# Instance norm over rows of 4096: one-pass statistics on VectorE for three rows of a tile, ScalarE takes the fourth

## The chip, the cores and the metric

The kernel runs on one core of one Trainium2 chip. The metric is device time in microseconds; before the change it is 4962.84 us, the median of three runs between 4960.73 and 4963.6.

## The reference

```python
batch, channels, length = 256, 256, 4096
x = np.random.randn(batch, channels, length).astype(np.float32)
eps = np.float32(1e-5)

def reference(x, eps):
    mean = np.mean(x, axis=2, keepdims=True)
    var = np.var(x, axis=2, keepdims=True)
    return ((x - mean) / np.sqrt(var + eps)).astype(np.float32)
```

There are 256 x 256 = 65,536 independent rows of 4096 floats. Each row needs its mean and its variance, and then one pass that subtracts and scales. Input and output are 1073.74 MB each.

## The kernel before

A tile is 128 partitions with K = 4 rows each: 512 rows, 64 KiB per partition, 8.39 MB in all. There are 128 tiles. Three buffers X[0] to X[2] hold tiles in SBUF; a tile is loaded into a buffer, normalised in place and stored from the same buffer. Nothing else of size is kept in SBUF; the output of the passes that are only summed goes to `junk` in PSUM.

Four engines run programs of their own, joined by semaphores that are written by hand:

- SyncE issues every DMA on one queue. In its loop (lines 202 to 205) it waits until tile t is done, issues its store (`store`, L164), waits until the store of tile t - 1 has landed, and issues the load of tile t + 2 into that buffer (`load`, L169). So the queue carries store, load, store, load, in that order, whole tiles at a time. Tile 0 is loaded, computed and stored in halves of two rows (L193, L180), and the last tile is stored in halves (L180).
- VectorE runs `vector_tile` once per tile. When the load has landed it takes four row sums (L89), each of which raises `means`. For each pair of rows it then waits for the standard deviations, takes their reciprocals (L97), forms the bias -mean/std (L99), and normalises the rows in place (L111): rows 0, 1 and 2 whole, and the last 1024 elements of row 3.
- ScalarE runs `scalar_tile`. For each row it waits for the row's sum and takes one Square pass over (sum - 4096 x) with an accumulated result (L136), which is the variance up to a factor; after each pair it takes the square root (L145). Finally it waits for `scaled` and normalises the first Q = 3072 elements of row 3 (L150).
- GpSimd only waits at the end for the last stores.

`done[s]` counts the finished pieces of a tile: K + 1 = 5 of them let the store go. The helper `take` (lines 67 to 69) waits for a semaphore and clears it, so that waits through it are shown under L69.

Of the kernel before, what the change touches and what calls it, by code (L numbers as in the profile page):

```python
# [10 lines left out]
def kernel(  # L11
# [6 lines left out]
    nc = tc.nc  # L18
    fp32 = mybir.dt.float32
    AX = mybir.AxisListType  # L20
    AF = mybir.ActivationFunctionType
    ALU = mybir.AluOpType
    P = 128
    K = 4
    BUFS = 3
    Q = 3072
# [2 lines left out]
    out_flat = out.flatten_outer_dims()  # L29
    n, d = x_flat.shape  # L30
    assert n % (P * K) == 0 and d & (d - 1) == 0

    ntiles = n // (P * K)
    x_t = x_flat.rearrange("(t p k) d -> t p k d", p=P, k=K)
# [3 lines left out]
    half = K // 2  # L38

    pool = ctx.enter_context(tc.tile_pool(name="pool", bufs=1))  # L40
# [2 lines left out]

    eps_tile = pool.tile([P, 1], fp32)

    junk = psum.tile([P, d], fp32)
    X = [pool.tile([P, K, d], fp32, name=f"x{s}") for s in range(BUFS)]
    total, ss, std, rstd, nbias = (
        [pool.tile([P, K], fp32, name=f"{name}{s}") for s in range(BUFS)]
        for name in ("total", "ss", "std", "rstd", "nbias")  # L50
    )
# [4 lines left out]
    loaded = [nc.alloc_semaphore(f"loaded{s}") for s in range(BUFS + 1)]  # L56
    stored = [nc.alloc_semaphore(f"stored{s}") for s in range(BUFS + 1)]
    own_v = nc.alloc_semaphore("own_v")
    own_a = nc.alloc_semaphore("own_a")
    means = nc.alloc_semaphore("means")  # L60
    stds = nc.alloc_semaphore("stds")
    scaled = nc.alloc_semaphore("scaled")
    done = [nc.alloc_semaphore(f"done{s}") for s in range(BUFS + 1)]
    ready = nc.alloc_semaphore("ready")
    issued = nc.alloc_semaphore("issued")

    def take(engine, sem, count):
        engine.wait_ge(sem, count)
        engine.sem_clear(sem)  # L69

    V, A, S, G = nc.vector, nc.scalar, nc.sync, nc.gpsimd

    def vector_tile(s, r0=0, k=K, ld=None, dn=None):

        x = X[s]
        ld = loaded[s] if ld is None else ld
        dn = done[s] if dn is None else dn
        dn = dn if isinstance(dn, list) else [dn] * K
        own = 0

        def mine(instruction):
            nonlocal own
            own += 1
            return instruction.then_inc(own_v, 1)

        if ld:
            take(V, ld, 16)
        for r in range(r0, r0 + k):
            V.reduce_sum(out=total[s][:, r : r + 1], in_=x[:, r, :], axis=AX.X).then_inc(means, 1)  # L89
        for b in range(r0, r0 + k, 2):  # L90
            c = slice(b, b + 2)
            final = b == r0 + k - 2
            if final:
                take(V, stds, (b - r0) // 2 + 1)
            else:
                V.wait_ge(stds, (b - r0) // 2 + 1)
            mine(V.reciprocal(out=rstd[s][:, c], in_=std[s][:, c]))  # L97
            V.wait_ge(own_v, own)
            mine(V.scalar_tensor_tensor(  # L99
                out=nbias[s][:, c], in0=total[s][:, c], scalar=-1.0 / d, in1=rstd[s][:, c], op0=ALU.mult, op1=ALU.mult  # L100
            ))
            if final:
                take(V, own_v, own)
            else:
                V.wait_ge(own_v, own)
            if final:
                V.sem_inc(scaled, 1)
            for r in range(b, b + 2):
                c = slice(r, r + 1)
                f = slice(Q, d) if r == r0 + k - 1 else slice(0, d)  # L110
                V.tensor_scalar(  # L111
                    out=x[:, r, f], in0=x[:, r, f], scalar1=rstd[s][:, c], scalar2=nbias[s][:, c],
                    op0=ALU.mult, op1=ALU.add,
                ).then_inc(dn[r], 1)

    def scalar_tile(s, r0=0, k=K, ld=None, dn=None):

        x = X[s]
        dn = done[s] if dn is None else dn
        last = r0 + k - 1  # L120
        own = 0

        def mine(instruction):
            nonlocal own
            own += 1
            return instruction.then_inc(own_a, 1)

        for r in range(r0, last + 1):
            c = slice(r, r + 1)
            if own:  # L130
                A.wait_ge(own_a, own)
            if r == last:
                take(A, means, k)
            else:
                A.wait_ge(means, r - r0 + 1)
            mine(A.activation(  # L136
                out=junk, in_=x[:, r, :], func=AF.Square, bias=total[s][:, c], scale=-float(d), accum_out=ss[s][:, c]
            ))
            if (r - r0) % 2:
                c = slice(r - 1, r + 1)  # L140
                if r == last:
                    take(A, own_a, own)
                else:
                    A.wait_ge(own_a, own)
                A.activation(  # L145
                    out=std[s][:, c], in_=ss[s][:, c], func=AF.Sqrt, bias=eps_tile, scale=1.0 / d**3
                ).then_inc(stds, 1)
        c = slice(last, last + 1)
        take(A, scaled, 1)
        A.activation(  # L150
            out=x[:, last, :Q], in_=x[:, last, :Q], func=AF.Identity, bias=nbias[s][:, c], scale=rstd[s][:, c]
        ).then_inc(dn, 1)

    def rows_of(ap, t):

        if isinstance(t, int):
            return ap[t]
        first, period, count, i = t
        ap = ap[first : first + period * (count - 1) + 1 : period]
        return ap[bass.ds(i, 1)].rearrange("o p k d -> p (o k) d")  # L160

    def store(s, t):
        take(S, done[s], K + 1)
        S.dma_start(out=rows_of(out_t, t), in_=X[s][:, :, :]).then_inc(stored[s], 16)  # L164

    def load(s, t, wait=True):
        if wait:
            take(S, stored[s], 16)
        S.dma_start(out=X[s][:, :, :], in_=rows_of(x_t, t)).then_inc(loaded[s], 16)  # L169

    def half_of(h):
        return slice(h * half, (h + 1) * half)

    def second(sems, s, h):
        return sems[BUFS] if h else sems[s]

    def store_half(s, t, h, count=half + 1):
        r = half_of(h)
        take(S, second(done, s, h), count)
        S.dma_start(out=out_t[t][:, r, :], in_=X[s][:, r, :]).then_inc(second(stored, s, h), 16)  # L180

    def halves(tile_fn, s):
        for h in range(2):
            tile_fn(s, h * half, half, second(loaded, s, h), second(done, s, h))

    last = ntiles - 1
    rounds = (ntiles - 5) // BUFS
    L0 = 2

    with tc.tile_critical():  # L190
        for h in range(2):
            r = half_of(h)
            S.dma_start(out=X[0][:, r, :], in_=x_t[0][:, r, :]).then_inc(second(loaded, 0, h), 16)  # L193
        load(1, 1, wait=False)
        store_half(0, 0, 0)
        store_half(0, 0, 1)
        load(2, 2, wait=False)
        store(1, 1)
        take(S, stored[BUFS], 16)
        load(0, 3)  # L200

        with S.Fori(0, rounds) as i:
            for t in range(L0, L0 + BUFS):
                store(t % BUFS, (t, BUFS, rounds, i))
                load((t + 2) % BUFS, (t + 2, BUFS, rounds, i))
        load(last % BUFS, last)
        store((last - 2) % BUFS, last - 2)
        store((last - 1) % BUFS, last - 1)
        store_half(last % BUFS, last, 0, half)
        store_half(last % BUFS, last, 1)  # L210
        S.sem_inc(issued, 1)
        take(G, issued, 1)
        for s in ((last - 2) % BUFS, (last - 1) % BUFS, last % BUFS, BUFS):
            take(G, stored[s], 16)

        V.memset(eps_tile, eps).then_inc(ready, 1)  # L216
        halves(vector_tile, 0)
        vector_tile(1)
        with V.Fori(0, rounds) as i:  # L219
            for j in range(BUFS):  # L220
                vector_tile((L0 + j) % BUFS)
        vector_tile((last - 2) % BUFS)
        vector_tile((last - 1) % BUFS)
        vector_tile(last % BUFS, dn=[done[last % BUFS]] * half + [done[BUFS]] * half)

        take(A, ready, 1)
        halves(scalar_tile, 0)
        scalar_tile(1)
        with A.Fori(0, rounds) as i:
            for j in range(BUFS):  # L230
                scalar_tile((L0 + j) % BUFS)
        scalar_tile((last - 2) % BUFS)
        scalar_tile((last - 1) % BUFS)
        scalar_tile(last % BUFS, dn=done[BUFS])


# [33 lines left out]
```

## Time and profile before

| | before |
|---|---|
| time, median of 3 | 4962.84 us |
| span of the profiled execution | 4959.6 us |
| DVE busy (VectorE) | 3292.8 us, 66%, 1537 instructions |
| ACT busy (ScalarE) | 2406.0 us, 49%, 1411 instructions |
| row sums, L89, DVE | 512 x 4412 ns |
| Square passes, L136, ACT | 512 x 3679 ns, and 187 ns for each read of the accumulator |
| normalising, L111, DVE | 383 x 2411 ns (4096 elements) and 129 x 808 ns (1024) |
| normalising, L150, ACT | 129 x 2950 ns (3072 elements) |
| roots, L145, ACT | 256 x 296 ns |
| reciprocals L97 and biases L99, DVE | 256 x 159 ns and 256 x 161 ns |

Busy time is that of instructions on an engine; what an engine spends in waits is not in it. The DMA has rows of its own on the page: the share of the sixteen DMA engines in forty equal slices of the span as tenths (9 means 90% or more), and for each queue the packets, the megabytes and the share of sixteen engines' span that the packets took. A row of the waits names who waited, for whom, the total, the count and the longest. A row of the table by stretches gives the stretch and its length, the busy time of DVE, ACT and POOL with the number of instructions, the granted clock, the DMA share and the GB/s.

### The profile page before, as it was taken

The page shows a single profiled execution, that of the slowest core. Times are in us where ns is not written, and L with a number is a line of the kernel's source. Part 1 is how long each engine was busy: PE and PEld are TensorE (multiplying, and loading weights), DVE is VectorE, ACT ScalarE, POOL GpSimd, SP SyncE. Part 2 cuts the span into 40 slices and gives each one's busy share as a digit, 9 for nine tenths or more (in the row PEclk, how much of TensorE's full clock was granted, in tenths as well). Part 3 has the DMA queues.
Part 4 walks back from the last instruction along what each step waited for, and adds up shares of the span by engine and source line. Part 5 has one row for each costly group of instructions (what it writes and reads, how often), then busy time and mean ns, then how long its engine had stood idle before and what let it go on. Part 6 is the DMA issues. An engine that isn't in the chain of part 4 may idle for free.

```text
span 4959.6 us, 5426 instructions
## 1 busy us (share of the span) xinstructions
DVE 3292.8 (66%) x1537; ACT 2406.0 (49%) x1411; POOL 0.2 (0%) x4
## 2 busy tenths in 40 slices
DVE  6666666666666666666666666666666666666666
ACT  4455444554445544455445544455444554445544
POOL 0000000000000000000000000000000000000000
DMA  9999999999999999999999999999999999999999
GB/s 422 431 431 432 434 432 431 437 434 431 436 434 432 436 434 433 436 433 436 434 433 436 434 432 436 434 433 435 434 433 436 433 433 437 433 433 436 434 432 413
DMA packets 37298, 2147.52 MB, mean 433 GB/s; under 512 B 4144, under 2 KB 4144, under 8 KB 4144
## 3 DMA queue, kind: packets, MB, share of 16 engines
q1 hardware_dynamic: 37296, 2147.50, 100.0%
q14 instruction: 2, 0.02, 0.0%
HBM read 1073.74 MB, written 1073.74 MB: 433 GB/s over the span
## 4 chain that ended last, share of the span: by engine, by line
DVE 62%; another core or an unknown queue 31%; issue 4%; DMA 2%; DVEq 0%; ACT 0%; SPq 0%; ACTq 0%
DVE total L89 44%; DVE x L111 17%; DMA x<-in_x_dram 1%; DVE nbias L99 1%; DMA out_dram<-x 1%; DVE rstd L97 1%; DVEq L69 0%; ACT junk L136 0%; DVEq L219 0%; ACT L145 0%; ACT std L145 0%; ACTq L69 0%; SPq L69 0%; SPq L265 0%
## 5 line engine op out<-in xcount | busy, mean ns | idle before, releaser
L89 DVE TENSOR_REDUCE total<-x 128x1 f32<-128x4096 f32 x512 | 2227.0, 4412 | 1591.6 <-DMA x<-in_x_dram 1591.6
L136 ACT ACTIVATE junk<-x,total 128x4096 f32<-128x4096 f32 x512 | 1883.6, 3679 | 2361.8 <-DVE total L89 2361.8
L111 DVE TENSOR_SCALAR x<-x,rstd,nbias 128x4096 f32<-128x4096 f32 (+1 forms) x512 | 1005.9, 2007 | 28.7 <-DVE nbias L99 24.0
L150 ACT ACTIVATE x<-x,nbias,rstd 128x3072 f32<-128x3072 f32 x129 | 380.6, 2950 | 145.0 <-DVEq L69 145.0
L136 ACT ACTIVATION_READ_ACCUMULATOR junk<-x,total 128x1 f32 x512 | 95.8, 187 | 0.0
L145 ACT ACTIVATE std<-ss,eps_tile 128x2 f32<-128x2 f32 x256 | 75.9, 296 | 19.0
L97 DVE RECIPROCAL rstd<-std 128x2 f32<-128x2 f32 x256 | 40.7, 159 | 10.3 <-ACT std L145 10.3
L99 DVE SCALAR_TENSOR_TENSOR nbias<-total,rstd 128x2 f32<-128x2 f32 x256 | 41.2, 161 | 8.8
L136 ACT ACT_TABLE_LOAD x1 | 1.3, 1283 | 1.2 <-DVE eps_tile L216 1.2
L145 ACT ACT_TABLE_LOAD x1 | 1.3, 1283 | 0.1
L216 DVE MEMSET eps_tile<- 128x1 f32 x1 | 0.1, 59 | 1.0 <-SPq L190 1.0
L251 POOL MEMSET const-bfloat16-1.0<- 128x1 bf16 x1 | 0.1, 103 | 0.0
L251 POOL MEMSET const-uint8-127<- 128x1 uint8 x1 | 0.1, 103 | 0.0
L251 POOL MEMSET const-float32-1.0<- 128x1 f32 x1 | 0.1, 100 | 0.0
L251 POOL MEMSET const-float32-0.0<- 128x1 f32 x1 | 0.1, 99 | 0.2 <-issue 0.2
## 6 DMA issues: line engine op xcount, KB each, us to landing
out_dram<-x SPq DMA_DIRECT2D x4, 4096.0 KB, 20.5
x<-in_x_dram SPq DMA_DIRECT2D x2, 4096.0 KB, 16.7
x<-in_x_dram SPq DMA_DIRECT2D x127, 50.3
out_dram<-x SPq DMA_DIRECT2D x126, 31.6
```

The source lines that it names most:

```text
L89: V.reduce_sum(out=total[s][:, r : r + 1], in_=x[:, r, :], axis=AX.X).then_inc(means, 1)
L97: mine(V.reciprocal(out=rstd[s][:, c], in_=std[s][:, c]))
L99: mine(V.scalar_tensor_tensor(out=nbias[s][:, c], in0=total[s][:, c], scalar=-1.0 / d, in1=rstd[s][:, c], op0=ALU.mult, op1=ALU.mult))
L111: V.tensor_scalar(out=x[:, r, f], in0=x[:, r, f], scalar1=rstd[s][:, c], scalar2=nbias[s][:, c], op0=ALU.mult, op1=ALU.add,).then_inc(dn[r ...
L136: mine(A.activation(out=junk, in_=x[:, r, :], func=AF.Square, bias=total[s][:, c], scale=-float(d), accum_out=ss[s][:, c]))
L145: A.activation(out=std[s][:, c], in_=ss[s][:, c], func=AF.Sqrt, bias=eps_tile, scale=1.0 / d**3).then_inc(stds, 1)
L150: A.activation(out=x[:, last, :Q], in_=x[:, last, :Q], func=AF.Identity, bias=nbias[s][:, c], scale=rstd[s][:, c]).then_inc(dn, 1)
L216: V.memset(eps_tile, eps).then_inc(ready, 1)
L251: nc = _bacc.Bacc("TRN2", target_bir_lowering=False, num_devices=1)
```

## The change

Two new functions, `vector_whole` and `scalar_whole`, take the place of `vector_tile` and `scalar_tile` for every tile but tile 0, which keeps the old ones in halves.

VectorE takes mean and variance of rows 0, 1 and 2 in one pass each: eight statistics instructions on 512 elements, and one that combines the eight results into mean and variance. ScalarE takes row 3 alone, and starts on it as soon as VectorE tells it through `started` that the load has landed: one Identity pass that accumulates the mean, and one Square pass for the variance. The square roots of row 3, of rows 0 and 1 together, and of row 2 are taken by ScalarE. VectorE forms the first three scales and biases together, takes row 2's statistics after them, and then normalises the first 3072 elements of row 3 and the whole of row 2. ScalarE normalises the whole of row 0, row 1 in two parts, and the last 1024 elements of row 3. The purpose is to divide the work so that neither engine waits for the other's statistics of every row, and to read each row of VectorE once for both moments.

A tile now has six pieces, and the store waits for K + 2. The last tile's first half waits for three.

```diff
+    R = d - Q
+    F = nc.vector.BN_STATS_FMAX
+    chunks = d // F
+    stats = pool.tile([P, K - 1, chunks, nc.vector.BN_STATS_DIM], fp32)
+    mv = [pool.tile([P, K, nc.vector.BN_AGGR_DIM], fp32, name=f"mv{s}") for s in range(BUFS)]
...
+    def vector_whole(s, dn=None):
...
+        def statistics(r):
+            for f in range(chunks):
+                mine(V.bn_stats(out=stats[:, r, f, :], in_=x[:, r, f * F : (f + 1) * F]))
+            V.wait_ge(own_v, own)
+            V.bn_aggr(out=mv[s][:, r + 1, :], in_=stats[:, r, :, :]).then_inc(means, 1)
...
+        take(V, loaded[s], 16)
+        V.sem_inc(started, 1)
+        statistics(0)
+        statistics(1)
+        c = slice(0, K - 1)
+        V.wait_ge(stds, 2)
+        scales(c)
+        mine(V.scalar_tensor_tensor(
+            out=nbias[s][:, c], in0=mv[s][:, c, 0], scalar=-1.0, in1=rstd[s][:, c], op0=ALU.mult, op1=ALU.mult
+        ))
+        V.wait_ge(own_v, own)
+        V.sem_inc(scaled, 1)
+        statistics(2)
+        normalise(K - 1, slice(0, Q), dn[1])
+        take(V, stds, 3)
+        mine(V.reciprocal(out=rstd[s][:, K - 1 :], in_=std[s][:, K - 1 :]))
+        take(V, own_v, own)
+        normalise(2, slice(0, d), dn[1])
...
+    def scalar_whole(s, dn=None):
...
+        take(A, started, 1)
+        A.activation(
+            out=junk, in_=last, func=AF.Identity, scale=1.0 / d, accum_out=mv[s][:, 0:1, 0]
+        ).then_inc(own_a, 1)
+        A.wait_ge(own_a, 1)
+        A.activation(
+            out=junk, in_=last, func=AF.Square, bias=mv[s][:, 0:1, 0], scale=-1.0, accum_out=ss[s][:, 0:1]
+        ).then_inc(own_a, 1)
+        take(A, own_a, 2)
+        root(slice(0, 1), ss[s][:, 0:1], 1.0 / d)
+        A.wait_ge(means, 2)
+        root(slice(1, K - 1), mv[s][:, 1 : K - 1, 1], 1.0)
+        take(A, scaled, 1)
+        normalise(0, slice(0, d), dn[0])
+        normalise(1, slice(0, R), dn[0])
+        take(A, means, 3)
+        root(slice(K - 1, K), mv[s][:, K - 1 :, 1], 1.0)
+        normalise(1, slice(R, d), dn[0])
+        normalise(K - 1, slice(Q, d), dn[1])
...
-        take(S, done[s], K + 1)
+        take(S, done[s], K + 2)
...
-        store_half(last % BUFS, last, 0, half)
+        store_half(last % BUFS, last, 0)
...
-                vector_tile((L0 + j) % BUFS)
+                vector_whole((L0 + j) % BUFS)
...
-                scalar_tile((L0 + j) % BUFS)
+                scalar_whole((L0 + j) % BUFS)
```

In both functions `normalise` works on one row: VectorE's subtracts the mean and multiplies by the scale, ScalarE's multiplies by the scale and adds the bias. The columns of `mv`, `std`, `rstd` and `nbias` are shifted by one, so that row 3 has column 0 and rows 0, 1 and 2 have columns 1, 2 and 3.

## Prediction

> **What bounds the kernel now.** I read the page's DMA rows first, because the engine rows (DVE 66%, ACT 49%) leave room on both engines, then what the engines and the DMA queue wait for, then one tile in the timeline. The rows of the page's parts 2 and 3:
>
> ```profile
> DMA  9999999999999999999999999999999999999999
> ...
> q1 hardware_dynamic: 37296, 2147.50, 100.0%
> ...
> HBM read 1073.74 MB, written 1073.74 MB: 433 GB/s over the span
> ```
>
> The packets of the one queue fill the sixteen DMA engines' whole span, from the first slice to the last, and the bytes are exactly one read of x and one write of the result: nothing is moved twice. The longest waits (total, times, longest):
>
> ```profile
> ACT junk L136 <- DVE total L89: 2361.8, 512, 18.3
> DVE total L89 <- DMA x<-in_x_dram: 1591.6, 126, 13.7
> ```
>
> VectorE waits 1591.6/126 = 12.6 us per tile for a load; ScalarE's wait for row sums lies inside VectorE's own work. Two stretches of one tile, engines idle and engines at work (length, busy DVE, ACT, POOL, clock, DMA share, GB/s):
>
> ```profile
> 2008.60:2020.90 12.30, 0.00 (x0) 0.00 (x0) 0.00 (x0) 1.00 0.98 426
> 2021.00:2047.00 26.00, 25.70 (x12) 18.75 (x11) 0.00 (x0) 1.00 1.01 439
> ```
>
> While no engine works, the DMA still moves 426 GB/s. The same tile in the timeline of the SyncE queue:
>
> ```profile
> 2008.58 0.34 SPq L164 DMA_DIRECT2D out_dram<-x  x1
> 2009.16 0.35 SPq L169 DMA_DIRECT2D x<-in_x_dram  x1
> 2047.15 0.34 SPq L164 DMA_DIRECT2D out_dram<-x  x1
> ```
>
> From issue to landing, in the answers for the loop's stores (L164), its loads (L169) and the four half-tile stores (L180), in this order:
>
> ```profile
> DMA to landing us min/median/max: 28.2/31.6/51.3
> ...
> DMA to landing us min/median/max: 34.2/50.3/52.4
> ...
> DMA to landing us min/median/max: 15.0/20.5/25.4
> ```
>
> Two transfers of 8.39 MB pass per tile, 19.3 us each. A store issued at 2008.58 lands 31.6 us later: it stands behind the 12.4 us that the load ahead of it still needs. The load issued with it lands after 50.3, which is 12.4 + 19.3 + 19.3. So whenever a store is issued, **the queue still holds 12.4 us of work**: the tile is finished that much sooner than the DMA needs it. The chain of waits puts DVE at 62% only because it follows the store's issue back to the engine; that is the order of the work and not what limits it.
>
> Average period: from store issue to store issue 38.64 us in mid-run, 16.777 MB / 38.64 = 434 GB/s; 128 x 38.64 = 4945.9 of the 4959.6 us span. The other 13.7 us: the three periods from 109.44 are 39.6 us and the next some twenty about 38.8, by my sum of the issue times 5.8 us over the mid-run pace, and 0.7 us near the end; 7.2 us are first issue, first landing and the last packets.
>
> [...]
>
> **The change part by part.** Times per tile, from the landing; 127 tiles take the new functions, tile 0 keeps the old ones.
>
> *VectorE's statistics.* Removed: four row sums, 17.40 us in the timeline for four. Added: 3 rows x 8 statistics instructions on 512 elements. The trace shows none. [...] I take 0.60, since the row sum is the nearest relative: one source, one pass, no result per element. Row: 8 x 0.60 + 0.08 for the last one's end + about 0.3 for aggregation and its wait (the small VectorE operations take 0.16) = 5.2 us.
>
> *ScalarE's statistics.* Removed: four Square passes. Added for row 3: one Identity and one Square pass with their accumulator reads, 2 x (3.68 + 0.19) = 7.7 us from the landing, beside VectorE's first two rows (10.4 us), so off the chain. Square, Sqrt and Identity already alternate with only two table loads in the whole run (1.3 us each, L136 and L145), so the new order of the same three costs none.
>
> *Roots, reciprocals, biases.* Root 0.30, hand-over 0.13, reciprocal and bias until the next big operation 0.55 (27.75 to 28.30 in the first tile): `scaled` rises near 10.4 + 0.05 + 0.30 + 0.13 + 0.55 = 11.4 us.
>
> *Normalising.* VectorE: third row's statistics 11.4 to 16.6; row 3's 3072 elements 1.88 (between 808 ns for 1024 and 2411 for 4096) to 18.4; reciprocal and wait 0.4; row 2 whole 2.41: end at 21.2. [...] Nothing else waits for that than the store, which now also needs both engines.
>
> Sum: tile finished about 21.2 us after landing instead of 26.05 (2021.0 to 2047.1). VectorE's busy time falls from 25.7 to about 19.8, ScalarE's from 18.75 to about 17.5. **All 4.9 us lie beside transfers**: the store comes into the queue with 12.4 + 4.9 = 17.3 us of work ahead instead of 12.4, and VectorE's wait for the next load grows by as much. The load issued with it needs the store before to have landed, 19.0 us after this tile's landing (31.6 - 12.6), so it too goes out at once. Effect per tile: 0.
>
> *Head and tail.* Tile 0 is unchanged; tile 1's store, issued at 74.32, stands behind load 2, which releases VectorE at 83.14: earlier does not help. At the end the last half store goes out at 4933.3 and lands after 25.4 us, though its 4.2 MB need only 9.7: about 15 us of other stores are ahead of it. Issuing it some 10 us earlier (two tiles run on end there, 2 x 4.9) lengthens its stay in the queue only. The store of the last first half now waits for one more increment, all three long before its turn. Effect: 0.
>
> **The rivals.**
> - *The statistics take VectorE over the DMA.* The chain has 24 x d + 6.8 us with d for one instruction; 26.05 + 12.6 = 38.6 is allowed. [...] It takes d over 1.33 us; at 1.5 a tile would cost 42.8 us and the kernel 128 x 42.8 = 5480. For: 24 instructions in place of 4, a price not shown. Against: more than two passes per element. Chance 2%.
> - *Other issue times upset the packets.* The early periods, 38.8 instead of 38.64, show that the same transfers can run 0.4% slower for a while. If that lasted, 105 more tiles x 0.16 = 17 us: 4980, slower. Against: 100 tiles in succession keep 38.64. Chance 4%.
> - *The head and tail gain.* If earlier stores spared the 6.5 us of drift: 4956. This is still inside 0.2% (9.9 us). Chance 8%.
> - *Less engine traffic frees the DMA.* [...] Against: the two stretches above, where idle engines bring no more GB/s. Chance 2%.
>
> **How the numbers follow.** The main case, chance 84%, is the old pace to about 0.1%: the time before, 4962.84, less a microsecond for what earlier stores may spare of the drift in the first periods. I predict 4962. The range 4955 to 4969 holds this case with a spread of 0.14% and the gain at head and tail; it leaves out the other three, 8%, and the edges of the main case. Within 0.2%: 84 + 8 = 92%, less 1 for both unclear edges, 91%; faster 3%; slower 6%.
>
> **What would show it.** Right: the DMA row still 9 throughout, 433 GB/s; the mid-run store-to-store period at 38.6; VectorE's wait for the load from 12.6 to about 17 us per tile; stores landing some 36 us after issue, loads some 55; statistics rows near 0.6 to 0.7 us each. Wrong: a period off 38.64, a DMA slice below 9, or an idle row of VectorE for the load that vanishes, which would mean that the engines had become the bound.

## The result, and the profile after

The changed kernel takes 4979.08 us (median of 6 runs, 4977.16 to 4980.29), the kernel before 4961.86 in the runs beside it: ratio 1.0034, 95% interval 1.0021 to 1.0047. It is slower by 17 us, and 4979 lies outside the forecast of 4955 to 4969.

Nearly everything that was forecast for the two engines came true. The page of the changed kernel, its two rows of the statistics, and the tile in the timeline:

```profile
L173 DVE BATCH_NORM_STATS2 stats<-x 128x6 f32<-128x512 f32 x3048 | 1837.7, 676 | 2264.6 <-DMA x<-in_x_dram 2245.7
...
L175 DVE BATCH_NORM_AGGREGATE mv<-stats 128x2 f32<-128x48 f32 x381 | 141.7, 372 | 13.1
```

```profile
2023.22 4.85 DVE L173 BATCH_NORM_STATS2 stats<-x 128x6 f32<-128x512 f32 x8 [17.99 <-DMA x<-in_x_dram]
...
2044.24 0.34 SPq L252 DMA_DIRECT2D out_dram<-x  x1
```

A statistics instruction takes 676 ns, eight in a row 4.85 us, and the tile is finished 21.0 us after landing. The waits and the same two kinds of stretch as before:

```profile
DVE stats L173 <- DMA x<-in_x_dram: 2245.7, 125, 19.2
```

```profile
2005.60:2023.10 17.50, 0.00 (x0) 0.00 (x0) 0.00 (x0) 1.00 0.99 427
2023.20:2044.20 21.00, 20.05 (x32) 17.30 (x11) 0.00 (x0) 1.00 1.02 440
```

VectorE waits 2245.7/125 = 18.0 us per tile for a load instead of 12.6, and is busy 20.05 us instead of 25.7. The issues to landing, for the stores (L252), the loads (L257) and the half stores (L268) in this order:

```profile
DMA to landing us min/median/max: 33.3/37.1/56.5
...
DMA to landing us min/median/max: 33.8/55.8/57.7
...
DMA to landing us min/median/max: 15.1/24.6/36.0
```

Stores enter the queue with 5.5 us more of work ahead of them, and it is of no use. The loss is in the DMA, and the page hardly shows it:

```profile
DMA  9999999999999999999999999999999999999998
...
q1 hardware_dynamic: 37296, 2147.50, 99.9%
...
HBM read 1073.74 MB, written 1073.74 MB: 431 GB/s over the span
```

The place to look is the issue times. A pair of store issues of the kernel before in mid-run, then three pairs of the changed kernel, early, in mid-run and late:

```profile
3013.24 0.34 SPq L164 DMA_DIRECT2D out_dram<-x  x1
...
3051.87 0.34 SPq L164 DMA_DIRECT2D out_dram<-x  x1
```

```profile
1036.38 0.34 SPq L252 DMA_DIRECT2D out_dram<-x  x1
...
1075.01 0.34 SPq L252 DMA_DIRECT2D out_dram<-x  x1
...
3015.12 0.34 SPq L252 DMA_DIRECT2D out_dram<-x  x1
...
3053.94 0.34 SPq L252 DMA_DIRECT2D out_dram<-x  x1
...
4725.84 0.34 SPq L252 DMA_DIRECT2D out_dram<-x  x1
...
4764.77 0.34 SPq L252 DMA_DIRECT2D out_dram<-x  x1
```

The period, from one store issue to the next, is 38.63 us in the kernel before; in the changed one it is 38.63, then 38.82, then 38.93. So the old pace of 38.64 holds for some 35 tiles, and is lost in two steps. In all issue times, the loss against 38.64 grows from tile 35 on and comes to 20.9 us at the end, against 3.0 us in the kernel before: about the 17 us of the result.

**Sixteen engines, not one queue.** In mid-run the DMA share is 1.00 and the mean 434 GB/s, as in the kernel before (its row stands first), while the period is already 38.82:

```profile
1300.00:3800.00 2500.00, 1661.33 (x778) 1211.10 (x710) 0.00 (x0) 1.00 1.00 434
...
1300.00:3800.00 2500.00, 1289.77 (x2056) 1113.53 (x709) 0.00 (x0) 1.00 1.00 434
```

Both can be true only if one of the sixteen DMA engines is late and the others run ahead. The trace shows it: each engine closes its share of a transfer with a write of 4 bytes (4144 = 259 transfers x 16, the page's count of packets under 512 B). I sorted the sixteen of each transfer; this is how far the last stands behind the median, in us, at one transfer of each of six tiles. (This table and the next ones are counted from the packet records of the traces.)

```
                    tile 20    40    60    80   100   120
before                  3.6   3.3   3.1   2.6   2.5   2.9
changed                 3.8   3.6   7.0  10.9  14.7  15.1
```

One engine falls behind by 0.19 us per tile, and its packets tell where. Each engine moves eight packets of 64 KB per whole-tile transfer (32384 packets = 253 such transfers x 16 x 8), each 2418 ns in nearly all cases. The late engine's packets, in ns over 2418, when it is the last:

```
                        store                           load
before, tile 122        6  3  0  0  0 10  0 28          2  0  0  0  9  4  1  1
changed, tile 72       15 18 14 23 33 18 14 23          2  0  2  2  9  2  2  2
```

Its loads cost 17 to 24 ns more than those of the others, in every kernel in which it could be followed; by that sign it can be told from the rest. Its **stores** cost about 50 ns more in the kernel before where it is the last (47 in the row above) and about 160 in the changed one (158 above): 0.158 + 0.023 = 0.18 us per tile, about the rate at which it falls behind. While it is not the last of the sixteen this costs nothing (the period is 38.63). Near tile 35 it becomes the last, and from then on SyncE's issues come at its pace, while the others go on at the old pace with what the queue still holds. From tile 90 on the leading engines are at the end of the queue; near tile 100 the late one is 15 us behind the median, and the period grows once more. Of the loss in this trace some 13 us come between tiles 35 and 100, and some 8 after them. In the kernel before the same kind of engine becomes the last only near tile 114.

### The profile page after: what moved, and what is told of

The parts are those of the page before. It is cut to its first block, busy times and chain, and to the rows that moved or that the text cites. A ratio compares the mean times of both kernels' runs of the same rounds, so it can differ in the third digit from the quotient of the medians.

```text
span 4978.0 us, 7839 instructions
## 1 busy us (share of the span) xinstructions
DVE 2570.8 (52%) x4077; ACT 2221.3 (45%) x1411; POOL 0.2 (0%) x4
## 2 busy tenths in 40 slices
DMA packets 37299, 2147.52 MB, mean 431 GB/s; under 512 B 4144, under 2 KB 4144, under 8 KB 4144
## 4 chain that ended last, share of the span: by engine, by line
DVE 47%; another core or an unknown queue 46%; issue 4%; ACT 1%; DMA 1%; DVEq 0%; SPq 0%; ACTq 0%
DVE stats L173 36%; DVE x L183 5%; DVE mv L175 3%; DMA x<-in_x_dram 1%; ACT std L214 1%; DVE rstd L203 1%; DVE rstd L178 0%; DVE nbias L195 0%; DVE total L95 0%; DVEq L75 0%; ACT junk L142 0%; ACT x L218 0%; DVEq L199 0%; DVEq L307 0%
## 5 line engine op out<-in xcount | busy, mean ns | idle before, releaser
L173 DVE BATCH_NORM_STATS2 stats<-x 128x6 f32<-128x512 f32 x3048 | 1837.7, 676 | 2264.6 <-DMA x<-in_x_dram 2245.7
L223 ACT ACTIVATE junk<-x 128x4096 f32<-128x4096 f32 x127 | 455.6, 3587 | 2245.2 <-DVEq L75 2245.2
L218 ACT ACTIVATE x<-x,nbias,rstd 128x4096 f32<-128x4096 f32 x508 | 1142.7, 2296 | 73.9 <-DVEq L199 73.9
L183 DVE TENSOR_SCALAR x<-x,mv,rstd 128x3072 f32<-128x3072 f32 x254 | 536.4, 2112 | 18.0
L227 ACT ACTIVATE junk<-x,mv 128x4096 f32<-128x4096 f32 x127 | 467.1, 3678 | 4.1
L175 DVE BATCH_NORM_AGGREGATE mv<-stats 128x2 f32<-128x48 f32 x381 | 141.7, 372 | 13.1
L142 ACT ACTIVATE junk<-x,total 128x4096 f32<-128x4096 f32 x4 | 14.7, 3677 | 21.0 <-DVE total L95 21.0
L95 DVE TENSOR_REDUCE total<-x 128x1 f32<-128x4096 f32 x4 | 17.5, 4412 | 12.1 <-DMA x<-in_x_dram 12.1
L156 ACT ACTIVATE x<-x,nbias,rstd 128x3072 f32<-128x3072 f32 x2 | 5.9, 2948 | 1.4 <-DVEq L75 1.4
L117 DVE TENSOR_SCALAR x<-x,rstd,nbias 128x4096 f32<-128x4096 f32 (+1 forms) x4 | 6.3, 1612 | 0.4 <-DVE nbias L105 0.4
## 6 DMA issues: line engine op xcount, KB each, us to landing
x<-in_x_dram SPq DMA_DIRECT2D x127, 55.8
out_dram<-x SPq DMA_DIRECT2D x126, 37.1
```

Source lines behind the costliest of these rows:

```text
L142: mine(A.activation(out=junk, in_=x[:, r, :], func=AF.Square, bias=total[s][:, c], scale=-float(d), accum_out=ss[s][:, c]))
L173: mine(V.bn_stats(out=stats[:, r, f, :], in_=x[:, r, f * F : (f + 1) * F]))
L175: V.bn_aggr(out=mv[s][:, r + 1, :], in_=stats[:, r, :, :]).then_inc(means, 1)
L183: V.tensor_scalar(out=x[:, r, f], in0=x[:, r, f], scalar1=mv[s][:, c, 0], scalar2=rstd[s][:, c], op0=ALU.subtract, op1=ALU.mult,).then_inc ...
L218: A.activation(out=x[:, r, f], in_=x[:, r, f], func=AF.Identity, bias=nbias[s][:, c], scale=rstd[s][:, c]).then_inc(sem, 1)
L223: A.activation(out=junk, in_=last, func=AF.Identity, scale=1.0 / d, accum_out=mv[s][:, 0:1, 0]).then_inc(own_a, 1)
```

## The experiments

Medians stand beside those of the kernel before in the same rounds: 4961.13 in the first group, 4961.27 in the second, 4961.71 in the third, 4960.39 in the last. "Finished" is the time from a tile's landing to its store. What is said of packets and engines comes from one traced run of each kernel; for `e6_more`, `e7_sems` and `e10_actsems` it is among the slowest (4977.94, 4991.03, 4987.69 us). One of the 24 runs of the kernel before in the first group took 4998.53 us; no trace of it was kept.

**First group: is it the place of the buffers, the earlier store, or the work on the engines?** The new tiles moved X[0] from byte 16544 of a partition to 17216.

`e1_layout`, the changed kernel with the new tiles behind the buffers:

```diff
-    stats = pool.tile([P, K - 1, chunks, nc.vector.BN_STATS_DIM], fp32)
-    mv = [...]
     junk = psum.tile([P, d], fp32)
...
         for name in ("total", "ss", "std", "rstd", "nbias")
     )
+    stats = pool.tile([P, K - 1, chunks, nc.vector.BN_STATS_DIM], fp32)
+    mv = [...]
```

> The changed kernel with the tiles stats and mv declared after the three buffers, so that X[0] begins at byte 16544 of each partition as in the kernel before, not at 17216. Theory 'issue time' (stores are issued 5 us earlier, so the sixteen DMA engines can run further apart, and one falls behind): the tile is finished 21 us after landing as in the changed kernel, so 4979 us and one engine's landings 13 to 15 us behind the median. Theory 'place' (the shift of the buffers slows one engine's transfers): 4962 us. Theory 'engine work' (statistics instructions and their semaphores disturb the DMA): 4979 us.

Measured: 4979.84 us, ratio 1.0039 (1.0025 to 1.0053).

`e2_pad`, the kernel before with its buffers moved:

```diff
+    pad = pool.tile([P, 168], fp32)
     junk = psum.tile([P, d], fp32)
...
+        V.memset(pad, 0.0)
```

> The kernel before with 672 unused bytes ahead of X[0], so that the buffers lie where the changed kernel has them. Theory 'issue time': 4962 us, tile finished 26 us after landing. Theory 'place': 4979 us. Theory 'engine work': 4962 us.

Measured: 4962.71 us, ratio 0.9997 (0.9983 to 1.0010). The place of the buffers is not the cause, shown from both sides.

`e3_late`, the changed kernel, finished later:

```diff
         take(V, own_v, own)
+        V.reduce_sum(out=total[s][:, 0:1], in_=x[:, 2, :], axis=AX.X)
         normalise(2, slice(0, d), dn[1])
```

> The changed kernel with one row sum of row 2, which nothing uses, on VectorE ahead of its last normalisation: the tile is finished 4.4 us later, about 25.4 us after landing, near the 26.05 of before. Theory 'issue time': 4962 us, or most of the way there. Theory 'place': 4979 us. Theory 'engine work': 4979 us, as all the statistics instructions are still there.

Measured: 4983.74 us, ratio 1.0047 (1.0030 to 1.0064); finished 25.3 us after landing. A later store doesn't bring the time back; it costs a little more.

`e4_early`, the kernel before, finished early:

```diff
+            w = [d, d, 3072, 128][r] if k == K else d
-            V.reduce_sum(..., in_=x[:, r, :], axis=AX.X)
+            V.reduce_sum(..., in_=x[:, r, :w], axis=AX.X)
...
+            w = [d, d, 2048, 128][r] if k == K else d
-                out=junk, in_=x[:, r, :], func=AF.Square, ...
+                out=junk[:, :w], in_=x[:, r, :w], func=AF.Square, ...
```

> The kernel before with the sums of rows 2 and 3 cut to 3072 and 128 elements and their Square passes to 2048 and 128 (the output of these rows is not the reference's): the tile is finished near 21 us after landing with the old instructions and buffers. Theory 'issue time': 4979 us and one engine lagging. Theory 'place': 4962 us. Theory 'engine work': 4962 us.

Measured: 4966.38 us, ratio 1.0009 (1.0000 to 1.0018), finished about 21.9 us after landing. The same number of instructions, only earlier (and some of them shorter), cost 5 of the 17 us. The late engine's stores cost 84 ns more here (about 50 before), which would fit more of the tile's instructions running during its store. Neither "place" nor "issue time" carries the bulk; the work on the engines remains.

**Second group: what of the work?** The changed kernel runs 7839 instructions by the page, the kernel before 5426.

`e5_nosem`, the changed kernel with fewer semaphore increments:

```diff
-                mine(V.bn_stats(...))
+                st = V.bn_stats(...)
+            mine(st)
```

> The changed kernel in which seven of the eight statistics instructions of each row raise no semaphore. Theory 'semaphores' (each increment by an instruction costs one DMA engine a few ns): 21 of some 40 increments per tile go, so most of the 17 us come back, 4965. Theory 'instructions' (each instruction that runs costs it, whatever it raises): 4979. Theory 'statistics' (the kind of instruction): 4979.

Measured: 4975.71 us, ratio 1.0028 (1.0017 to 1.0039); the late engine's stores cost 136 ns more. 21 increments that ride on instructions cost 22 ns, about 1 ns each. The 3 us between the two medians are inside the intervals of the ratios.

`e6_more`, the kernel before with 24 short instructions:

```diff
+    scratch = pool.tile([P, 24], fp32)
...
             V.reduce_sum(...).then_inc(means, 1)
+            for i in range(6 if k == K else 0):
+                V.memset(scratch[:, 6 * r + i : 6 * r + i + 1], 0.0)
```

> The kernel before with 24 more VectorE instructions per tile, memsets of one element per partition into a scratch tile that nothing reads, six after each row sum, without semaphores; the tile is finished about 1.5 us later. Theory 'instructions': about the same number is added as in the changed kernel (20 per tile), so near 4979, one DMA engine lagging early. Theory 'semaphores': 4962. Theory 'statistics': 4962.

Measured: 4970.73 us, ratio 1.0021 (1.0011 to 1.0030); the late engine's stores cost 83 ns more, some 110 where the engine is last. Instructions without semaphores, and of another kind, do it too.

`e7_sems`, the kernel before with 24 increments that VectorE's sequencer makes alone:

```diff
+    spare = nc.alloc_semaphore("spare")
...
             V.reduce_sum(...).then_inc(means, 1)
+            for i in range(6 if k == K else 0):
+                V.sem_inc(spare, 1)
+            if k == K:
+                V.sem_clear(spare)
```

> The kernel before with 24 semaphore increments per tile that VectorE's sequencer makes by itself, six after each row sum, and a clear: no more work on the engine. Theory 'semaphores': near 4979. Theory 'instructions', if those of the sequencer count as well: near 4979; if only those of the engine count: 4962. Theory 'statistics': 4962.

Measured: 4985.63 us, ratio 1.0046 (1.0029 to 1.0062). This run decides most: engine work, schedule within a tile and bytes are those of the kernel before, and 24 us are lost. The added line in the window of one tile that landed at 2022.4:

```profile
L92 DVEq EVENT_SEMAPHORE  x24: 21/21/21, 2022.4 to 2024.9; - x24
```

The sequencer runs ahead of the row sums and makes all 24 within 2.5 us of the landing, not spread over the sums as the program order suggests. They cost the late engine some 90 ns in each store. That alone is not the 24 us: the engine becomes the last near tile 53, only some 6 of the 33 us that this trace loses against 38.64 are gone by tile 60, and the other 27 follow with the leading engines at the end of the queue. This second limit is the subject of the last group.

`e8_sum`, the changed kernel with one row sum in place of eight statistics instructions:

```diff
-            for f in range(chunks):
-                mine(V.bn_stats(...))
+            mine(V.reduce_sum(out=mv[s][:, r + 1, 0:1], in_=x[:, r, :], axis=AX.X))
             V.wait_ge(own_v, own)
-            V.bn_aggr(...)
+            V.tensor_scalar(
+                out=mv[s][:, r + 1, 0:2], in0=x[:, r, 0:2], scalar1=0.0, scalar2=1.0, ...
```

> The changed kernel in which the eight statistics instructions of a row are one row sum, and the aggregation is one small operation that writes constants (mean and variance of three rows are left out): the same schedule and order, tile finished some 20 us after landing, 21 fewer instructions and increments per tile. Theory 'instructions': 4962 to 4966, as in the kernel before made early. Theory 'semaphores': the same. Theory 'statistics': the same. Another cause (ScalarE's new order, row-wise normalising): 4979.

Measured: 4968.25 us, ratio 1.0014 (1.0007 to 1.0021); the late engine's stores cost 85 ns more, as in the early version of the kernel before. Taking out 21 instructions per tile from an otherwise nearly equal schedule returns 11 of the 17 us. What remains, 7, is near the cost of an early finish (5 above).

**Third group: when, where from, and how much?**

`e9_lastsems`, the same increments at the end of the tile:

```diff
                 ).then_inc(dn[r], 1)
+        if k == K:
+            for i in range(4):
+                for j in range(6):
+                    V.sem_inc(spare, 1)
+                V.sem_clear(spare)
```

> The kernel before with the 24 spare semaphore increments of VectorE's sequencer (and four clears) behind the tile's last normalisation, 22 to 26 us after landing, where the DMA engine that lands last is already loading, and no longer among the row sums, where it stores. Theory 'stores only' (instructions cost that engine time only while it stores): 4961 to 4965. Theory 'any time': near 4985, as with the increments among the sums.

Measured: 4961.62 us, ratio 0.9999 (0.9990 to 1.0008). The added line in one tile that landed at 2020.5:

```profile
L119 DVEq EVENT_SEMAPHORE  x21: 21/21/21, 2043.4 to 2045.7; - x21
```

(The trace lists 21 of the 24 as instructions of their own.) 23 to 25 us after landing the last DMA engine is through with its store (19.3 us) and loads. The increments are free there. What differs from `e7_sems` is when they run.

`e10_actsems`, the increments on ScalarE, six and a clear after each Square pass:

```diff
             mine(A.activation(out=junk, ..., func=AF.Square, ...))
+            if k == K:
+                for i in range(6):
+                    A.sem_inc(spare, 1)
+                A.sem_clear(spare)
```

> The kernel before with 24 spare semaphore increments (and four clears) per tile on ScalarE's sequencer, six after each Square pass, 4 to 22 us after landing. Theory 'instructions of any engine': 4975 to 4985. Theory 'VectorE's stream alone': 4962.

Measured: 4978.80 us, ratio 1.0033 (1.0022 to 1.0045). So the cost is not confined to VectorE's instruction stream. The added line in a tile that landed at 2022.5:

```profile
L142 ACTq EVENT_SEMAPHORE  x24: 17/17/17, 2027.0 to 2040.5; - x24
```

`e12_halfsems`, half of the increments of `e7_sems`:

```diff
-            for i in range(6 if k == K else 0):
+            for i in range(3 if k == K else 0):
```

> The kernel before with 12 spare semaphore increments of VectorE's sequencer per tile, three after each row sum (24 of them gave 4985.63). Theory 'instructions', the loss grows with their number: about half of the 24 us, 4970 to 4976. If there is a threshold: 4962 or 4985.

Measured: 4974.53 us, ratio 1.0025 (1.0016 to 1.0035): 13 of the 24 us. Between 0, 12 and 24 increments there is no threshold. The packets of the late engine, as above, one store of each:

```
                                            store
ScalarE, four groups over the tile           0  3 16 23 14 47  0 47
VectorE, 12 within the first us or so       70  0  0  9  0  9  4 28
VectorE, 24 at the end of the tile           0  3  0  2  0 23  0 18
```

A packet lasts 2.4 us, so from the start of the store the first runs from 0 to 2.4 us and the third from 4.8 to 7.3; VectorE starts on the tile 0.5 to 0.6 us after the last engine's store begins (median 0.50 in the kernel before, 0.63 in the changed one). On this scale ScalarE's groups run at 5.1, 9.5, 13.8 and 18.2 us. The excess is in the third packet, in the fourth and fifth (the second group lies across their turn at 9.7), in the sixth and in the eighth. VectorE's twelve cost 70 - 6 = 64 ns of the first packet here and 53 - 6 in many other tiles, 4 to 5 ns for each increment with the clears counted in. **In these traces the packet that pays is the one in transit while the instruction runs.**

`e11_shift`, the changed kernel, all of it later:

```diff
         take(V, loaded[s], 16)
+        for r in range(2):
+            mine(V.reduce_sum(out=total[s][:, r : r + 1], in_=x[:, r, :], axis=AX.X))
+        V.wait_ge(own_v, own)
         V.sem_inc(started, 1)
```

> The changed kernel with two row sums that nothing uses ahead of the statistics, so that all of its other work begins about 9 us after landing and the tile is finished at about 30: half of the statistics instructions then run while the last DMA engine loads. Theory 'stores only': 4965 to 4972. Theory 'any time': 4979 to 4984. Theory 'issue time' in its first form (the later the store is issued, the better): below 4962.

Measured: 5010.66 us (4971.4 to 5017.4), ratio 1.0087 (1.0062 to 1.0112). A miss for each theory: moving half of the statistics out of the store should have helped, and it cost 32 us more (one of the seven runs, 4971.4, was as fast as hoped). A second limit had to be there.

**Last group: the room between finish and period.** VectorE's wait for a load is the room: what the queue still holds when the tile's store is issued.

`e13_wait` and `e15_wait2`, the kernel before with one or two row sums that nothing uses, ahead of its own (the range is 1 in the first and 2 in the second):

```diff
+        for r in range(1 if k == K else 0):
+            V.reduce_sum(out=scratch[:, r : r + 1], in_=x[:, r, :], axis=AX.X)
         for r in range(r0, r0 + k):
             V.reduce_sum(out=total[s][:, r : r + 1], ...).then_inc(means, 1)
```

> The kernel before with one row sum that nothing uses ahead of its own: the tile is finished 30.4 us after landing, which leaves 8.2 us of queue, still more than the spread of 6.4 us that the sixteen DMA engines have in the kernel before. Theory 'room for the spread': 4961 to 4965. Theory 'late finish costs by itself': near 4980.

Measured: 5012.07 us (4993.92 to 5016.91), ratio 1.0095 (1.0073 to 1.0117). The room, and three store issues in the timeline:

```profile
DVE scratch L90 <- DMA x<-in_x_dram: 1089.0, 125, 10.0
```

```profile
3006.17 0.34 SPq L167 DMA_DIRECT2D out_dram<-x  x1
...
3045.01 0.34 SPq L167 DMA_DIRECT2D out_dram<-x  x1
...
3084.20 0.34 SPq L167 DMA_DIRECT2D out_dram<-x  x1
```

> The kernel before with two such row sums: finished 34.8 us after landing, which leaves 3.8 us of queue, less than the spread of 6.4 us. Theory 'room for the spread': the leading DMA engines run dry from the first tiles on, period 39 us or more, 4990 to 5040. If only a drained queue (finish over 38.6 us) costs, as the prediction had it: 4962.

Measured: 5063.89 us, ratio 1.0206 (1.0189 to 1.0223). Its room:

```profile
DVE scratch L90 <- DMA x<-in_x_dram: 592.2, 124, 8.3
```

Two instructions per tile, a tile finished with 4.8 us to spare on the mean, and 103 us lost. Both runs are slower than the theory of the room had said. In the store issues of `e13_wait` the periods are uneven, 38.84 and 39.19 us. Over the kernels, the distance from the first to the last DMA engine (the spread) stops at 1.3 to 2.4 us less than the room at the six tiles, and at 0.9 to 1.9 less over all transfers:

```
                 room = VectorE's wait    widest spread at the six tiles
e15_wait2        592.2/124  =  4.8         3.2
e13_wait        1089.0/125  =  8.7         7.4 once, then 6.1 to 6.4
e11_shift       1159.9/125  =  9.3         7.6
before          1591.6/126  = 12.6         5.7   (limit not reached)
e7_sems         1620.1/126  = 12.9        10.8
e3_late         1706.8/125  = 13.7        11.4
e14_earlysems   2155.3/126  = 17.1        14.9
changed         2245.7/125  = 18.0        15.6
```

That is up to one packet. The kernel before has a spread of 4.5 to 5.7 us of its own at the six tiles (6.4 at most over all transfers), under a limit of some 10 or more (12.6 less a packet of 2.4); one more row sum brings the limit to between 6 and 8 (8.7 less 0.9 to 2.4), and the engines to it. My expectation compared the spread with the whole room and left out this packet. The packet was read from the traces afterwards; no run was made to test it.

What is lost at the limit is mostly not idle time. The share of the DMA engines stays at 1.00 and the rate falls, from 434 GB/s in the kernel before to 429 (`e13_wait`, first) and 425 (`e15_wait2`):

```profile
1300.00:3800.00 2500.00, 1919.58 (x832) 1199.54 (x704) 0.00 (x0) 1.00 1.00 429
...
1300.00:3800.00 2500.00, 2176.07 (x886) 1181.94 (x694) 0.00 (x0) 1.00 1.00 425
```

In this stretch the packets of 64 KB take 2446 and 2453 ns on the mean instead of 2418, 1.2% and 1.4% more, where the periods are 1.3% and 2.1% longer. Single packets take up to 1800 ns longer; why was not tested.

`e14_earlysems`, `e4_early` with the increments of `e7_sems`:

```diff
             V.reduce_sum(..., in_=x[:, r, :w], axis=AX.X).then_inc(means, 1)
+            for i in range(6 if k == K else 0):
+                V.sem_inc(spare, 1)
```

> The kernel before with cut sums and Square passes (rows 2 and 3 not the reference's; 4966.38 without more) and 24 spare semaphore increments of VectorE per tile among the sums: finished 22 us after landing, 16.7 us of queue left. Theory of both limits: the last DMA engine falls behind as with the same increments in the kernel before (4985.63), but the spread reaches the room later, so 4975 to 4982. With the instructions alone as the cause: 4985 or more.

Measured: 4986.42 us, ratio 1.0047 (1.0031 to 1.0064). More room saved nothing, against the 4975 to 4982 of the theory of both limits: its last engine is already 14.7 us behind at tile 80. With one engine losing time in every store, more room (17.1 us against 12.9 in `e7_sems`) did not mend that loss.

No version beats the kernel before. In mid-run its packets take 2418 ns nearly without exception; what a better one could gain in the loop is a part of its first periods.

## Why the prediction was wrong

**Right, by its own steps.** One statistics instruction 0.60 us forecast, 4.85/8 = 0.61 measured (the 0.60 was my estimate, which no view of before shows; one by itself takes 676 ns, and eight in a row overlap by (8 x 676 - 4850)/7 = 80 ns at each join, as the row sums before did: 4 x 4.412 us against 17.40); tile finished 21.2 us after landing, 21.0; VectorE busy 19.8, 20.05; ScalarE 17.5, 17.30 (this, too, was my estimate: of its normalising only the 2950 ns for 3072 elements had been shown, and it now takes 3801, 2933 and 1226 ns for 4096, 3072 and 1024); VectorE's wait 17, 18.0; stores landing after 36 us, 37.1, loads 55, 55.8. That this gain would lie beside transfers and bring nothing was right (`e4_early` shows that it even costs), and so was the pace of 38.6, for 35 tiles.

**The step that failed** is "Effect per tile: 0". Measured, the effect is 0 up to tile 35, then 0.19 us per tile, and some 0.3 after tile 100. The step treated the queue as one channel that is either full or not, at 434 GB/s. It needed two things that no view before the change had shown: that the sixteen DMA engines keep together, and that instructions cost none of them anything. The second rested on two stretches, 439 GB/s with the engines at work and 426 without. These are means over sixteen. One engine that loses 0.16 us in a store of 19.3 us loses 0.8%, and the mean 0.05%; these means could not show it, and once that engine is the last, it sets the period. The forecast's own sign of being wrong, "a period off 38.64", is what came.

**The premise behind it** was that the engines' work and the transfers do not slow each other. The mean rate of the changed kernel's two stretches still shows no slowing (427 GB/s idle, 440 busy). As a reason to price instructions at nothing it did not hold in these runs: increments that read and write no tile slowed one engine's stores by 4 to 5 ns each (64 ns for twelve in `e12_halfsems`).

**The rivals.** The second, "other issue times upset the packets", gave 4980 and was put at 4%. That its number came so near is in good part luck; its reason was right only in part. It let all packets run 0.4% slower for 105 tiles. Instead one engine is slower for 92, and of its cost the earlier finish alone makes 5 us (`e4_early`), and the added instructions the larger part (11 us in `e8_sum`). The chances were too narrow because the case for "no change" counted a hundred equal periods of a kernel whose VectorE instructions were about to grow from 1537 to 4077.

**Also wrong, in the first rival:** the allowance of 38.6 us for a tile. `e15_wait2` is finished inside it and loses 2%. By the table above, the room that counts is smaller by the spread of the DMA engines and up to one packet.

**Open.** Why an instruction lengthens the packets of one engine's stores was not found. All runs here are recorded by the profiler, and whether the records themselves are part of it was not tried. The costs would fit that too, for they follow the number of instructions that the trace lists: 21 instructions less gave 11 us back (`e8_sum`), 21 increments less that ride on instructions gave 3 (`e5_nosem`). So it is not shown that the loss exists without the profiler. Why packets grow longer at the second limit is open as well. The first periods of the kernel before, 39.6 us, have long packets too: 2440 ns on the mean between 110 and 230 us, with the sixteen 1.4 to 3.9 us apart. No run tested whether the cause is the same. Why an early finish moves more of the cost into the store fits the times at which instructions run, but was not tested apart.

## What to carry to other kernels

When a kernel is bound by its DMA, look at the last of the sixteen engines and at the period of the issues, not at the mean share: a row of nines hides an engine that loses 0.8%. Here work on idle engines was not free (24 increments per tile cost 24 us), so count the instructions that run while stores are in transit, try few long ones (one row sum in place of eight statistics instructions gave 11 us back), and put what can wait behind the stores (the same 24 increments there: 4961.62 us against 4961.71). In these runs that was worth up to 0.5%, under the profiler. Keep the wait for the next load well above the spread of the DMA engines, here 12.6 us of a 38.6 us period against 5.7; with 8.7 the same kernel lost 1%.

## What the runs showed of the hardware

- Among the sixteen DMA engines one paid for instructions: 4 to 5 ns in its store for an increment made by a sequencer (VectorE's or ScalarE's), about 1 ns for an increment that rides on an instruction, and nothing that shows in the time while it loads (4961.62 against 4961.71 us). With 24 such increments per tile the run lost 24 us on VectorE and 17 on ScalarE; in the trace on VectorE most of it came after the leading DMA engines had reached the end of the queue.
- In `e7_sems` VectorE's sequencer made semaphore increments far ahead of the long instructions before them: 24 within 2.5 us, though they stand between four row sums of 4.4 us.
- In seven kernels the distance between the first and last DMA engine stopped at the room less 0.9 to 1.9 us, at most a packet of 2.4 us. In the two made to run at this limit it cost 0.4 and 0.8 us per tile of 38.6 (51.7 and 103.5 us over 128 tiles), mostly in longer packets (2446 and 2453 ns against 2418).
